# A two-layer decoder trunk: VectorE instead of GpSimd for a layer norm's affine step, ScalarE and GpSimd instead of VectorE for eight convolution taps

## The chip, the cores and the metric

The kernel runs on one core of one Trainium2 chip. The metric is the device time of one execution, in microseconds (us). The engines are named as the profile names them: PE is TensorE (PEld its weight loads), DVE is VectorE, ACT is ScalarE, POOL is GpSimd, SP is SyncE, which issues the DMAs here. Each engine runs its own instructions strictly in the order in which the built program has them, and waits on semaphores for the others.

## The reference

The trunk has two layers over x of 512 tokens and 1024 channels, all in float32. Cut to what matters here:

```
def reference(x, ...):
    for layer in range(2):
        mix = even_mixer(x, ...) if layer % 2 == 0 else odd_mixer(x, ...)
        x = layer_norm(ALPHA * x + mix, ln_mix_g[layer], ln_mix_b[layer])
        x = layer_norm(ALPHA * x + swiglu(x, ffn_w_in[layer], ffn_w_out[layer]),
                       ln_ffn_g[layer], ln_ffn_b[layer])

def odd_mixer(x, w_in, forget_b, dw_w, dw_b, cn_g, cn_b, w_out):
    p = x @ w_in                      # q, k, v of 8 heads of 64; 8 forget gates; 2 x 512 for the convolution
    log_f = log_sigmoid(p[forget gates] + forget_b)
    y_c = forgetting_attention(q, k, v, log_f)
    y_d = conformer_conv(p[the last 1024], dw_w, dw_b, cn_g, cn_b)
    return concatenate([y_c, y_d]) @ w_out

def forgetting_attention(q, k, v, log_f):   # causal; logits q.k/8 + cum[t] - cum[s]; softmax; times v
def conformer_conv(p_d, ...):
    h = p_d[:, :512] * sigmoid(p_d[:, 512:])
    h = causal_dwconv(h, dw_w) + dw_b       # 31 taps on each of 512 channels
    return silu(layer_norm(h, cn_g, cn_b))  # the norm over channels
```

## The kernel before

**Arithmetic.** Matrix products are made from split operands: each float32 operand is written as a high part, rounded to the type in which TensorE multiplies (`split`, lines 85 to 88: ACT copies, DVE or POOL subtracts), and a low part, the remainder. `mm3` (lines 90 to 93) then sums three products, so the matmuls of a projection stand at lines 91, 92 and 93 in the profile.

**Stages.** The four calls at the end of `trunk` run one after the other: `even_mixer`, `ffn(0)`, `odd_mixer`, `ffn(1)`. In `ffn` a part of the products is made by a Strassen scheme (line 389). The tokens lie in four tiles x_74 to x_77 of 128 tokens by 1024 channels.

**The norm behind the first FFN.** `norm` (lines 210 to 220) leaves the tiles as (x - mean) * rstd, without factor and bias; the transposed copy that the odd mixer's projections read gets them there (`transpose_x`). The residual at the odd mixer's end needs them on the token tiles too. That is the affine step: `late_affine` (lines 203 to 208) calls `affine_steps` (lines 194 to 201), which loads factor and bias (`gb`, 512 KB each, spread over the partitions, line 198) into two buffers of the weight pool `wt`, which has eight, and returns 16 instructions of 128x512, a multiplication and an addition for each half of each tile (line 200). They are given out with a priority that is shifted against program order (`tc.high_priority(offset=-CP)`, CP = 900), as are the convolutions.

**The odd mixer.** It begins with the four column blocks j of the convolution's input. `conv` (lines 737 to 758) makes the 31 taps of one block. The last `GT[j]` of them are made by ACT and POOL: ACT multiplies (lines 753 and 748) and POOL adds each product to `convs` (line 749). `prod` holds two products in each of these blocks, so ACT's product i waits for POOL's sum i - 2. The other taps go on DVE: ACT makes the first in PSUM (line 743), DVE adds the rest in place (line 755) and then the two sums (line 758). With GT = (0, 31, 0, 4), blocks 0 and 2 are wholly DVE's, block 1 wholly ACT's and POOL's, and block 3 is shared. Then come the forget gates, their cumulated sums (`cumulate`, lines 858 to 875, into `aug`), and the values. DVE's last row of `aug` (line 875) goes by DMA into the operand tiles (line 928).

**The eight heads.** Lines 1092 to 1107 write out TensorE's order by hand: for every head the ten steps of SEQ.

```
SEQ = "S0 F0 T0 S1 S2 F1 F2 W T1 F3"
```

S are the scores of the 128-row blocks (b=3; b=2 and 0; b=1), with L945, L946, L947 on PE, the row maxima (L952) and reciprocals (L955) on DVE and the exponentials and scaling (L954, L956) on ACT. T are transposes of the probabilities (L970), T0 those of the head before; they are split into th and tl (L87 on ACT, L88 on DVE). W is the weighted sum of the values (L986). F are quarters of the projection of queries and keys of the head after next (`qk_proj`; its operands are made by L917 and L920 on ACT, L918 and L921 on DVE, and copied across partitions by the DMAs of L922 and L923), or in the last two heads parts of the output projection. The operand tiles are three, qk0 to qk2, used in turn.

Other work hangs on a pair (head, step). `CS = [(4, 0), (4, 6), (5, 0), (5, 6)]` places `conv_stats`, the norm of the convolution over channels: PE transposes (L1005) into the PSUM bank "cv", of which there is one; DVE takes the statistics (L1008, L1009, L168), POOL a power (L169), and DVE normalizes out of the bank (L1011). CW places `conv_swish` (L1025 to L1034), which uses the same bank. XG places the affine step; `extra` holds all of these (lines 1082 to 1088).

**What sets the order.** PE's order here is the written one. On the other engines the scheduler decides, by its own estimates of time and by priority; so the place of an instruction in a queue can differ from where the code gives it out.

Of the kernel before, what the change touches and what calls it, by code (L numbers as in the profile page):

```python
# [45 lines left out]
DFIRST = 2  # L46
DG = 1
XA = 2
XG = (3, 8)
FPOS = 3  # L50
GT = (0, 31, 0, 4)
PRE = "C Q0 A0 Q1 V00 V01 A1 V10 V11"
SEQ = "S0 F0 T0 S1 S2 F1 F2 W T1 F3"
CS = [(4, 0), (4, 6), (5, 0), (5, 6)]
# [7 lines left out]
def trunk(ctx, tc, x, ev_w_in, ev_conv_w, ev_pool_w, ev_pool_scale, ev_w_out, od_w_in,  # L62
# [131 lines left out]
    def affine_steps(g, b, eng):  # L194

        gb = [wtp.tile([P, D], F32, tag="wt", name="gb") for _ in range(2)]
        for dst, v in zip(gb, (g, b)):
            nc.sync.dma_start(dst, v.partition_broadcast(P))
        return [lambda t=t, cs=slice(c * 512, (c + 1) * 512), v=v, op=op:
                eng.tensor_tensor(xs[t][:, cs], xs[t][:, cs], v[:, cs], op=op)  # L200
                for t in range(NT) for c in range(2) for v, op in zip(gb, (ALU.mult, ALU.add))]

    def late_affine(g, b, eng):

        steps = affine_steps(g, b, eng)
        with tc.high_priority(offset=-CP):
            for step in steps:
                step()
# [27 lines left out]
    class OutProj:  # L236
# [13 lines left out]
        def step(self, t, i, ws, part=None):  # L250

            q = slice(t * P, (t + 1) * P)
            for acc, cols in self.accs[t] if part is None else [self.accs[t][part]]:
                for kk in range(2):
                    lh, ll = self.lhs(2 * self.order[i] + kk)
                    mm3(acc, lh[:, q], ll[:, q], ws[0][:, kk, cols], ws[1][:, kk, cols],
                        i == 0 and kk == 0, i == len(self.order) - 1 and kk == 1)
# [461 lines left out]
    def odd_mixer():  # L719
# [3 lines left out]
        V = nc.vector  # L723
        G = nc.gpsimd
        with tc.tile_pool(name="odd", bufs=1) as op:
# [11 lines left out]
            def conv(hp, j):  # L737

                acc, n = convs[:, j, :], KCONV - GT[j]
                tap = lambda i: par[:, j, 4 + i:5 + i]  # L740
# [341 lines left out]
            extra = {}  # L1082
# [2 lines left out]
            for j in range(4):  # L1085
                extra.setdefault(CW[j], []).append(lambda j=j: conv_swish(j))

            extra.setdefault(XG, []).append(lambda: late_affine(ln_ffn_g[0], ln_ffn_b[0], G))
            run = lambda key: [f() for f in extra.get(key, ())]
            ctx2.enter_context(tc.manual_schedule(engines={mybir.EngineType.PE}))  # L1090
            pt, seq = {}, SEQ.split()
# [33 lines left out]
    even_mixer()  # L1125
    ffn(0)
    odd_mixer()
    ffn(1)

# [22 lines left out]
```

## Time and profile before

| | us |
|---|---|
| median of the three runs | 1078.4 |
| the runs | 1077.87, 1078.4, 1086.64 |
| the profiled execution | 1077.13 |
| its span | 1075.4 |
| mean granted clock of TensorE | 0.99 |
| heads 0 to 7, from the first head's rest to the last | about 592 to 680 |

A row of the groups view has line, engine, operation, output<-input, shape and count, then busy time in us and the mean duration in ns, then the idle time of the engine just before and what ended it. In the timeline the columns are start and duration in us, engine, line and operation; a bracket gives the engine's idle time before the instruction and its releaser. A row of the waits view reads: who, waited for whom: us in total, times, longest.

### The profile page before, as it was taken

What the parts mean: (1) busy time and instruction counts of PE and PEld (TensorE: products, weight loads), DVE (VectorE), ACT (ScalarE), POOL (GpSimd) and SP (SyncE); (2) the same over time, 40 slices, a digit from 0 to 9 for tenths busy, and PEclk for the clock granted to TensorE, in tenths of its full rate; (3) what the DMA queues carried; (4) which work ended last, traced back from release to release, by engine and by line L of the source; (5) the groups of instructions that cost most, each with busy time, mean ns of one, the idle gap of its engine ahead of it and who ended that gap; (6) DMA issues with size and microseconds to landing.
All of it is one profiled execution on the core that took longest, in us unless ns stands there. A gap on an engine that the chain in (4) does not pass through costs nothing.

```text
span 1075.4 us, 16367 instructions
## 1 busy us (share of the span) xinstructions
PE 1040.8 (97%) x6649; PEld 934.3 (87%) x6649; DVE 742.5 (69%) x1028; ACT 482.6 (45%) x711; POOL 177.1 (16%) x162
## 2 busy tenths in 40 slices
PE   8999999999799999999999999999999799999997
PEld 8888899899788999988978777889899788999986
DVE  3845476988653788757579978466888663788756
ACT  4433243554321455433576888533555321455420
POOL 1000300000000000012499972710000000000003
PEclk9999999999899999999999999999999899999999
DMA  6523502530423340460333332411530433340522
GB/s 197 148 84 113 157 1 63 174 99 21 157 98 118 119 136 21 137 177 21 80 86 91 96 104 59 121 36 42 183 110 2 163 111 117 118 138 21 164 72 79
DMA packets 112457, 108.49 MB, mean 101 GB/s; under 512 B 5256, under 2 KB 93880, under 8 KB 112382
## 3 DMA queue, kind: packets, MB, share of 16 engines
q1 hardware_dynamic: 110462, 105.35, 31.8%
q10 hardware_dynamic: 1920, 2.10, 0.6%
q8 instruction: 52, 0.85, 0.3%
q14 instruction: 23, 0.19, 0.1%
HBM read 103.17 MB, written 2.10 MB: 98 GB/s over the span
## 4 chain that ended last, share of the span: by engine, by line
PE 76%; DVE 10%; ACT 5%; issue 3%; DMA 2%; POOL 2%; ACTq 0%; SPq 0%; POOLq 0%; DVEq 0%
PE fl L389 13%; PE fl L91 8%; PE fl L93 8%; PE fl L92 8%; PE sc L389 6%; PE sc L93 5%; PE sc L92 5%; PE sc L91 5%; DVE sw L381 4%; DVE sum L370 2%; PE py L92 2%; PE py L91 2%; PE py L93 2%; PE cv L93 2%; PE cv L91 2%
## 5 line engine op out<-in xcount | busy, mean ns | idle before, releaser
L87 ACT ACTIVATE w<-raw 128x1024 fp32r<-128x1024 f32 x104 | 109.4, 1058 | 197.4 <-PE sc L92 64.2
L389 PE MATMUL fl<-T,sw 128*128 128x256 f32 x1296 | 162.0, 281 | 14.2 <-ACT u L397 11.1
L389 PEld LDWEIGHTS fl<-T,sw 128*128 128x128 f32 x1296 | 155.5, 191 | 16.8 <-ACT u L397 12.2
L88 DVE TENSOR_TENSOR w<-raw,w 128x1024 fp32r<-128x1024 f32 x77 | 93.9, 1223 | 84.0 <-ACT w L87 83.4
L88 POOL TENSOR_TENSOR w<-raw,w 128x1024 fp32r<-128x1024 f32 x27 | 64.9, 2415 | 417.9 <-ACT w L87 404.2
L377 ACT ACTIVATE sw<-sum 128x1024 fp32r<-128x1024 f32 x72 | 76.1, 1062 | 102.9 <-DVE sum L370 77.3
L381 DVE TENSOR_TENSOR sw<-sum,sw 128x1024 fp32r<-128x1024 f32 x72 | 87.8, 1219 | 24.7 <-ACT sw L377 24.7
L389 PE MATMUL sc<-xh,sw 128*128 128x256 f32 x576 | 104.5, 277 | 0.0
L389 PEld LDWEIGHTS sc<-xh,sw 128*128 128x128 f32 x576 | 89.7, 188 | 0.1
L381 DVE TENSOR_TENSOR sw<-q,sw 128x1024 fp32r<-128x1024 f32 x54 | 65.4, 1220 | 29.2 <-ACT sw L377 29.1
L389 PE MATMUL sc<-xl,sw 128*128 128x256 f32 x288 | 79.8, 277 | 0.0
L169 POOL TENSOR_TENSOR rs<-rs,neghalf 128x1 f32<-128x1 f32 x20 | 13.6, 678 | 401.8 <-DVE rs L168 401.8
L377 ACT ACTIVATE sw<-q 128x1024 fp32r<-128x1024 f32 x54 | 56.4, 1051 | 44.2 <-DMA q<-in_ffn_w_in 44.2
L91 PE MATMUL fl<-w,hh 128*128 128x512 f32 (+1 forms) x176 | 67.8, 385 | 0.5 <-ACT w L87 0.5
L93 PE MATMUL fl<-w,hl 128*128 128x512 f32 (+1 forms) x176 | 67.6, 384 | 0.0
L92 PE MATMUL fl<-w,hh 128*128 128x512 f32 (+1 forms) x176 | 67.6, 384 | 0.0
L755 DVE SCALAR_TENSOR_TENSOR cv<-hp,par,cv 128x512 f32<-128x512 f32 x84 | 63.1, 751 | 5.8 <-ACT cv L743 4.5
L370 DVE TENSOR_TENSOR sum<-q,q 128x1024 f32<-128x1024 f32 x36 | 43.9, 1218 | 25.5 <-DMA q<-in_ffn_w_in 25.5
L91 PE MATMUL sc<-xh,w 128*128 128x256 f32 (+1 forms) x168 | 55.1, 332 | 0.0
L92 PE MATMUL sc<-xl,w 128*128 128x256 f32 (+1 forms) x168 | 55.0, 329 | 0.0
L389 PE MATMUL fl<-xh,sw 128*128 128x256 f32 x288 | 53.2, 279 | 1.9 <-DVE sw L381 1.9
L93 PE MATMUL sc<-xh,w 128*128 128x256 f32 (+1 forms) x168 | 54.8, 328 | 0.0
(419 smaller groups left out, 2638.8 us busy)
## 6 DMA issues: line engine op xcount, KB each, us to landing
q<-in_ffn_w_in SPq DMA_DIRECT2D x72, 512.0 KB
raw<-in_ffn_w_out SPq DMA_DIRECT2D x44, 512.0 KB
raw<-in_od_w_in SPq DMA_DIRECT2D x20, 512.0 KB
raw<-in_ffn_w_in SPq DMA_DIRECT2D x16, 512.0 KB
raw<-in_ev_w_in SPq DMA_DIRECT2D x15, 512.0 KB
raw<-in_ev_w_out SPq DMA_DIRECT2D x8, 512.0 KB
raw<-in_od_w_out SPq DMA_DIRECT2D x8, 512.0 KB
qk<-qk SPq DMA_DIRECT2D x16, 128.0 KB
```

The costliest lines, as they stand in the source:

```text
L87: nc.scalar.activation(hi, src, AF.Copy)
L88: (eng or nc.vector).tensor_tensor(lo, src, f32(hi), op=ALU.subtract)
L91: nc.tensor.matmul(acc, lh, rh, start=start, stop=False)
L92: nc.tensor.matmul(acc, lh, rl, start=False, stop=False)
L93: nc.tensor.matmul(acc, ll, rh, start=False, stop=stop)
L169: nc.gpsimd.tensor_tensor(rs[:, 1:2], rs[:, 0:1], neghalf, op=ALU.pow)
L370: nc.vector.tensor_tensor(raw[name], raw[a], raw[b], op=ALU.add)
L377: nc.scalar.activation(g["A"][name][0], g["raw"][self.LEFT[name]], AF.Copy)
L381: nc.vector.tensor_tensor(lo, g["raw"][self.LEFT[name]], f32(hi), op=ALU.subtract)
L389: nc.tensor.matmul(acc, l[:, k, cols], r[:, k, :], start=start and i == k == m == 0, stop=stop and i == 1 and k == 3 and m == 2, skip_grou ...
L755: V.scalar_tensor_tensor(acc if i == KCONV - 1 else part, hp[:, i:i + S], tap(i), part, op0=ALU.mult, op1=ALU.add)
```

## The change

Two numbers and one engine change:

```
-XG = (3, 8)
+XG = (6, 8)
 FPOS = 3
-GT = (0, 31, 0, 4)
+GT = (0, 31, 0, 12)
...
-            extra.setdefault(XG, []).append(lambda: late_affine(ln_ffn_g[0], ln_ffn_b[0], G))
+            extra.setdefault(XG, []).append(lambda: late_affine(ln_ffn_g[0], ln_ffn_b[0], V))
```

V is VectorE and G is GpSimd. The affine step is now given out behind step 8 of head 6 instead of head 3, and on VectorE. In block 3 of the convolution twelve taps instead of four are made by ACT and POOL, and 18 instead of 26 products are added by DVE (line 755). No other line changes.

## The prediction

> **What bounds the kernel now.** First the page's busy times, then TensorE's idle time by stage in the windows view, then TensorE's waits in the odd mixer.
>
> ```profile
> span 1075.4 us, 16367 instructions
> PE 1040.8 (97%) x6649; PEld 934.3 (87%) x6649; DVE 742.5 (69%) x1028; ACT 482.6 (45%) x711; POOL 177.1 (16%) x162
> ```
>
> ```profile
> 580.00:592.40 12.40, 9.32 (x77) 8.68 (x75) 10.12 (x18) 8.25 (x16) 11.89 (x10) 1.00 0.33 86
> 592.40:632.40 40.00, 38.51 (x199) 30.85 (x200) 35.58 (x79) 34.09 (x85) 37.47 (x31) 0.96 0.27 79
> 632.40:680.00 47.60, 44.52 (x257) 35.93 (x257) 37.14 (x88) 40.16 (x92) 15.89 (x12) 1.00 0.26 80
> 680.00:800.00 120.00, 117.92 (x777) 107.19 (x776) 84.37 (x114) 53.42 (x75) 20.94 (x12) 1.00 0.35 106
> ```
>
> ```profile
> PE sc L947 <- DMA qk<-aug: 3.1, 1, 3.1
> PE tp L970 <- ACT pr L956: 1.5, 4, 0.6
> PE cv L1005 <- DVE sm L955: 0.6, 1, 0.6
> ```
>
> TensorE (PE) is busy for 97% of the span and its order is the same in both kernels, so the time moves only by what makes PE wait. The columns of a windows row are the stretch, its length, then busy time of PE, PEld, DVE, ACT, POOL, the granted clock, and DMA. In heads 0 to 3 (592.4 to 632.4) PE idles 40.00 - 38.51 = 1.5 us, in heads 4 to 7 (to 680) 3.1 us. More than that nothing can be won here. GpSimd (POOL) and VectorE (DVE) are the full engines of heads 0 to 3: 37.5 and 35.6 of 40 us.
>
> **The change, part by part.** It takes eight taps of conv j=3 and the 16 affine steps and swaps their engines.
>
> ```profile
> L749 POOL TENSOR_TENSOR convs<-convs,prod 128x512 f32<-128x512 f32 x33 | 42.5, 1297 | 3.1 <-ACT prod L748 2.0 <-PE fl L92 0.3
> L748 ACT ACTIVATE prod<-hp,par 128x512 f32<-128x512 f32 x33 | 23.5, 719 | 9.4 <-POOL convs L749 9.3
> L755 DVE SCALAR_TENSOR_TENSOR cv<-hp,par,cv 128x512 f32<-128x512 f32 x84 | 63.1, 751 | 5.8 <-ACT cv L743 4.5
> L200 DVE TENSOR_TENSOR x<-x,gb x32: 681/684/695, 288.7 to 873.5; 128x512 f32<-128x512 f32 x32
> L200 POOL TENSOR_TENSOR x<-x,gb x16: 1269/1282/1295, 605.4 to 627.9; 128x512 f32<-128x512 f32 x16
> ```
>
> Work on DVE: 8 x 0.751 = 6.0 us less before head 2, and 16 x 0.65 = 10.4 us more later. Here 0.65 us is the step of back-to-back affine instructions, from the row of six below: (3.94 - 0.68) / 5. On POOL: 16 x 1.28 = 20.5 us less, 8 x 1.30 = 10.4 us more. On ScalarE (ACT): 8 x 0.72 = 5.8 us more. Were the engines free where this falls, PE would notice nothing. Where it falls decides.
>
> **Head 4, the large term.** The schedule puts the sixteen L200 not in the last heads, but into head 4, all between the statistics of the first conv transposes (L1008) and the instruction that reads their PSUM bank for the last time (L1011). DVE before, from L1008 on (qk is an operand tile, tl the low half of a transposed probability block, x_74 to x_77 the four token tiles):
>
> ```order
> L1008 BN_STATS cst<-cv 128x6
> L955 RECIPROCAL sm<-sm 128x1
> L1009 BN_AGGR mv<-cst 128x2
> L168 TENSOR_SCALAR rs<-mv 128x1
> L921 TENSOR_TENSOR qk_5265<-fl,qk_5265 64x512
> L952 TENSOR_REDUCE nm<-sc 128x1
> L88 TENSOR_TENSOR tl<-tp,th 128x512
> L88 TENSOR_TENSOR tl<-tp,th 128x384
> L955 RECIPROCAL sm<-sm 128x1
> L952 TENSOR_REDUCE nm<-sc 128x1 x2
> L1011 TENSOR_SCALAR npair<-cv,mv,rs 128x512
> ```
>
> The same place on DVE in the changed kernel, its first part:
>
> ```order
> L955 RECIPROCAL sm<-sm 128x1
> L200 TENSOR_TENSOR x_74<-x_74,gb 128x512 x2
> L1009 BN_AGGR mv<-cst 128x2
> L200 TENSOR_TENSOR x_75<-x_75,gb 128x512
> L921 TENSOR_TENSOR qk_5273<-fl,qk_5273 64x512
> L200 TENSOR_TENSOR x_75<-x_75,gb 128x512
> L200 TENSOR_TENSOR x_76<-x_76,gb 128x512 x2
> L200 TENSOR_TENSOR x_77<-x_77,gb 128x512 x2
> L952 TENSOR_REDUCE nm<-sc 128x1
> L200 TENSOR_TENSOR x_74<-x_74,gb 128x512
> L168 TENSOR_SCALAR rs<-mv 128x1
> L88 TENSOR_TENSOR tl<-tp,th 128x512
> ```
>
> And DVE's rows that follow directly:
>
> ```order
> L200 TENSOR_TENSOR x_74<-x_74,gb 128x512
> L88 TENSOR_TENSOR tl<-tp,th 128x384
> L200 TENSOR_TENSOR x_75<-x_75,gb 128x512 x2
> L200 TENSOR_TENSOR x_76<-x_76,gb 128x512 x2
> L200 TENSOR_TENSOR x_77<-x_77,gb 128x512 x2
> L955 RECIPROCAL sm<-sm 128x1
> L952 TENSOR_REDUCE nm<-sc 128x1
> L1011 TENSOR_SCALAR npair<-cv,mv,rs 128x512
> ```
>
> Sixteen steps now stand ahead of the second L955 and of L1011. Behind them wait the softmax of the remaining rows of head 4, and PE: the conv bank has one buffer, so PE's second set of conv transposes (the L1005 ahead of the weighted sum, L986) can't start until L1011 has read the first, and PE runs in order. In the trace of before this wait is already without slack:
>
> ```profile
> 632.46 0.40 PE L945 MATMUL sc<-qk 128*128 128x512 f32 x1
> 633.05 0.60 PE L1005 MATMUL cv<-ident,convs 128*128 128x128 f32 x4
> ...
> 640.31 0.63 PE L1005 MATMUL cv<-ident,convs 128*128 128x128 f32 x4 [0.61 <-DVE sm L955]
> ```
>
> ```profile
> 635.84 0.16 DVE L955 RECIPROCAL sm<-sm 128x1 f32<-128x1 f32 x1 [0.45 <-ACT pr L954]
> ...
> 636.46 0.69 DVE L921 TENSOR_TENSOR qk<-fl,qk 64x512 fp32r<-64x512 f32 x1 [0.19 <-ACT qk L920]
> 637.18 0.56 DVE L952 TENSOR_REDUCE nm<-sc 128x1 f32<-128x384 f32 x1
> 637.70 1.16 DVE L88 TENSOR_TENSOR tl<-tp,th 128x512 fp32r<-128x512 f32 x2
> 638.77 0.15 DVE L955 RECIPROCAL sm<-sm 128x1 f32<-128x1 f32 x1
> 638.84 0.60 DVE L952 TENSOR_REDUCE nm<-sc 128x1 f32<-128x128 f32 x2
> 639.36 0.81 DVE L1011 TENSOR_SCALAR npair<-cv,mv,rs 128x512 f32<-128x512 f32 x1
> ```
>
> L1011 ends at 640.17, and PE goes on at 640.31, 0.14 us later. (The wait's named releaser, L955, ended nearby; the bank's reader fits by code and by time.)
>
> When may the first L200 start? The factors come by DMA into buffers of the eight-deep weight pool, and the queue of SP now issues them behind other heads' transfers (qk_5271 to qk_5273 belong to heads 0/3/6, 1/4/7, 2/5). Before, on SP:
>
> ```order
> L98 DMA raw<-in_od_w_out 128x2x512
> L928 DMA qk_5263<-aug 2x512 x2
> L198 DMA gb<-in_ln_ffn_g 128x1024
> L198 DMA gb<-in_ln_ffn_b 128x1024
> L922 DMA qk_5265<-qk_5265 64x512
> ```
>
> SP in the changed kernel:
>
> ```order
> L923 DMA qk_5272<-qk_5272 64x512
> L928 DMA qk_5271<-aug 2x512 x2
> L198 DMA gb<-in_ln_ffn_g 128x1024
> L198 DMA gb<-in_ln_ffn_b 128x1024
> L922 DMA qk_5273<-qk_5273 64x512
> ```
>
> They moved from ahead of head 2's operand copies to ahead of head 5's. Their buffers held the weights of head 5, so they wait for the last projection of head 3, as they waited in before for the last of head 0:
>
> ```profile
> 601.20 0.34 SPq L198 DMA_DIRECT2D gb<-in_ln_ffn_g  x1
> 601.24 0.39 PE L945 MATMUL sc<-qk 128*128 128x512 f32 x1
> 605.44 1.29 POOL L200 TENSOR_TENSOR x<-x,gb 128x512 f32<-128x512 f32 x1 [0.90 <-DMA gb<-in_ln_ffn_g]
> 868.04 3.94 DVE L200 TENSOR_TENSOR x<-x,gb 128x512 f32<-128x512 f32 x6
> ```
>
> Issue lay 0.04 us before the next head's first scores, first use 4.24 us later. Head 4's scores start at 632.46, so L200 starts at 632.42 + 4.24 = 636.66, which is 0.8 us behind L955 and costs DVE little. From there L1011 ends after 16 x 0.65 + 0.1 (L1009) + 0.72 (L921) + 0.52 (L952) + 0.1 (L168) + 1.07 (two tl) + 0.07 (L955) + 0.26 (one L952) + 0.81 = 14.05 us, at 650.71. PE restarts at 650.85 instead of 640.31: **+10.5 us**. Nothing covers it: all that PE could do meanwhile stands behind the L1005. Bounds: below, 16 x 0.65 less the 1.9 us that DVE idled in head 4 (8.5); above, another 1.5 us if the DMA meets the output projection's loads (12.0).
>
> **The clock after it.** A pause of this length isn't in the trace; the nearest are 3.1 and 5.5 us.
>
> ```profile
> 592.32 0.50 PE L947 MATMUL sc<-qk 68*128 68x512 f32 x1 [3.08 <-DMA qk<-aug]
> 275.83 0.58 PE L389 MATMUL fl<-T,sw 128*128 128x256 f32 x1 [5.53 <-ACT u L397]
> 275.83:279.40 3.57, 3.57 (x17) 3.57 (x18) 3.57 (x4) 0.89 (x1) 0.00 (x0) 0.54 0.62 213
> 592.32:596.76 4.44, 4.44 (x17) 3.43 (x17) 3.82 (x8) 2.80 (x6) 4.36 (x5) 0.62 0.35 100
> ```
>
> After them the granted clock was 0.54 over 3.57 us and 0.62 over 4.44 us: 3.57 x 0.46 = 1.6 and 4.44 x 0.38 = 1.7 us lost. I take **+1.7**; bounds 0 (the slowed matmuls lie beside a wait for softmax) and 2.
>
> [...]
>
> **Heads 0 to 3, the small terms.** ACT around the cumulated forget gates (aug) has one tap more ahead of L874, whose output DVE finishes and a DMA carries to PE, which waited 3.08 us for it. Before, on ACT:
>
> ```order
> L872 ACTIVATE aug<-py 8x512
> L748 ACTIVATE prod<-hp,par 128x512
> L743 ACTIVATE cv<-hp,par 128x512
> L87 ACTIVATE wqh<-raw 128x8x64 x2
> L874 ACTIVATE aug<-py 8x512
> ```
>
> ACT in the changed kernel:
>
> ```order
> L872 ACTIVATE aug<-py 8x512
> L748 ACTIVATE prod<-hp,par 128x512
> L743 ACTIVATE cv<-hp,par 128x512
> L87 ACTIVATE wqh<-raw 128x8x64 x2
> L748 ACTIVATE prod<-hp,par 128x512
> L874 ACTIVATE aug<-py 8x512
> ```
>
> ```profile
> 586.90 0.71 ACT L748 ACTIVATE prod<-hp,par 128x512 f32<-128x512 f32 x1
> 587.51 0.76 ACT L743 ACTIVATE cv<-hp,par 128x512 f32<-128x512 f32 x1
> ```
>
> The step from one to the next is 587.51 - 586.90 = 0.61, so **+0.6**. For the rest I take **0**: DVE's relief can return the 1.5 us of idle in these heads, and eight more L748, in line with the softmax on ACT, can cost as much; the bounds are -1.5 and 8 x 0.66 = +5.3, with 0.66 = 9.3 us in 14 waits of L748 for POOL. The near end is likelier: POOL loses its affine between those taps.
>
> **Sum.** 10.5 + 1.7 + 0.6 = 12.8 us. The profiled execution took 1077.13 us (span 1075.4 and 1.7 around it): 1077.1 + 12.8 = 1089.9, say **1090.0**. It lies 1.3 us under the median of before (1078.4), inside the runs' own scatter.
>
> **Rivals.** (1) *The pause is partly repaid*: while PE stands, ACT, POOL and the loads catch up, and the waits behind it vanish. For it: PE idles 3.1 us in heads 4 to 7 (0.6 of it the wait that grows) and 2.1 from 680 to 800. Against it: most are chains through the same one bank, not backlog. At most 2.5 + 2.1 = 4.6 back: 1085.3. (2) *ScalarE and GpSimd pace the first heads*: every L748 waits for the sum two taps earlier, with softmax queued behind it on ACT. For it: POOL at 37.5 of 40 us; against it: DVE is freer just there. 12.8 + 5.3 gives 1095. (3) *Not slower*: the affine is covered. This needs PE to come to its second L1005 of head 4 only at about 650, so that DVE's 14 us pass beside other PE work; then the relief stays, -1.5, and the time is 1075.6. Against it: PE stood there at 639.7, 0.6 us early, and conv work before head 4 would have to be 10 us late. That the title's "last heads" were true would also cover some, but the order shows head 4.
>
> **How the numbers follow.** Forecast 0.68, partly repaid 0.14, paced 0.12, covered 0.06. The forecast's own bounds are about 1087 to 1093; the range is widened to 1084.5 and 1095.0 for (1) and (2). A measurement of this kernel can tell about 1%, that is 10.8 us, from no change: the forecast lies 1 us beyond that line. Two thirds of its chance (0.46) and all of "paced" (0.12) are slower by over 1%, 0.6 rounded; covered gives faster by at most 0.3%, so faster by over 1% gets 0.02, and 0.38 is left for within 1%.
>
> **What the changed profile would show.** One wait of PE L1005 for DVE of about 11 us at 640 to 651, a dozen or more L200 on DVE just before it, PE clock near 0.6 for four us after it; the wait for qk<-aug at 3.7; PE's idle in heads 0 to 3 within 1.5 us of now. It would be wrong if that L1005 waits under 8 us, if the affine runs in another head, or if ACT's waits for convs grow by 5 us with PE behind them.

## The result, and the profile after

| | before | after |
|---|---|---|
| median of the runs, us | 1078.2 (6 runs, 1077.47 to 1086.64) | 1091.9 (6 runs, 1090.24 to 1095.03) |
| the profiled execution, us | 1077.13 | 1090.53 |
| its span, us | 1075.4 | 1088.8 |

The change makes the kernel slower: the ratio of the times is 1.0116, with a 95% interval of 1.0083 to 1.0149 (the two medians alone would give 1.0127). The medians differ by 13.6 us, the profiled executions by 13.4.

The page's head and its rows of the moved work show that the work went where the change says: VectorE has the 16 affine steps more and 8 L755 less, GpSimd the reverse, ScalarE 8 L748 more.

```profile
span 1088.8 us, 16388 instructions
PE 1043.5 (96%) x6649; PEld 937.7 (86%) x6649; DVE 747.5 (69%) x1036; ACT 487.2 (45%) x719; POOL 167.0 (15%) x154
...
L755 DVE SCALAR_TENSOR_TENSOR cv<-hp,par,cv 128x512 f32<-128x512 f32 x76 | 57.1, 752 | 5.8 <-ACT cv L743 4.5
```

VectorE's busy time grew by 5.0 us in 747, and TensorE's share of the span fell by one point. Nothing in these averages looks like 13 us. The windows view by stage does: the same stages as in the prediction, from the first heads to head 4, and then the stretch from TensorE's restart to the first scores of head 5.

```profile
593.00:633.70 40.70, 38.34 (x200) 31.03 (x200) 30.55 (x70) 37.00 (x90) 28.41 (x22) 0.96 0.29 86
633.70:651.15 17.45, 7.24 (x43) 5.65 (x41) 15.74 (x32) 6.24 (x13) 1.47 (x2) 0.79 0.23 76
651.15:655.99 4.84, 4.84 (x21) 4.41 (x22) 3.10 (x9) 2.60 (x8) 2.00 (x2) 0.69 0.35 112
```

TensorE idles 2.4 us of heads 0 to 3 (1.5 before) and 10.2 of 17.45 us in head 4, where VectorE is busy for 15.7. The waits view of TensorE for the odd mixer names it:

```profile
PE cv L1005 <- DVE npair L1011: 10.2, 1, 10.2
PE sc L947 <- DMA qk<-aug: 3.8, 1, 3.8
PE sc L945 <- ACT pr L954: 1.2, 1, 1.2
...
PE sc L945 <- DMA qk<-qk: 0.8, 1, 0.8
```

One wait of 10.2 us has taken the place of one of 0.6; the wait for aug grew by 0.7, and two small ones are new. VectorE's timeline in head 4 shows what L1011 stood behind (start, duration, instruction; in brackets the idle time and its releaser):

```profile
636.55 0.14 DVE L955 RECIPROCAL sm<-sm 128x1 f32<-128x1 f32 x1
637.80 1.29 DVE L200 TENSOR_TENSOR x<-x,gb 128x512 f32<-128x512 f32 x2 [1.11 <-DMA gb<-in_ln_ffn_g]
...
640.41 3.09 DVE L200 TENSOR_TENSOR x<-x,gb 128x512 f32<-128x512 f32 x5
643.53 0.56 DVE L952 TENSOR_REDUCE nm<-sc 128x1 f32<-128x384 f32 x1
...
646.33 3.69 DVE L200 TENSOR_TENSOR x<-x,gb 128x512 f32<-128x512 f32 x6
649.94 0.15 DVE L955 RECIPROCAL sm<-sm 128x1 f32<-128x1 f32 x1
650.01 0.27 DVE L952 TENSOR_REDUCE nm<-sc 128x1 f32<-128x128 f32 x1
650.20 0.80 DVE L1011 TENSOR_SCALAR npair<-cv,mv,rs 128x512 f32<-128x512 f32 x1
```

And TensorE's timeline at the same place:

```profile
633.70 0.40 PE L945 MATMUL sc<-qk 128*128 128x512 f32 x1
...
640.55 0.39 PE L93 MATMUL fl<-xh,wql 128*128 128x512 f32 x1
651.15 1.08 PE L1005 MATMUL cv<-ident,convs 128*128 128x128 f32 x4 [10.21 <-DVE npair L1011]
```

Factor and bias are there 4.10 us after head 4's first scores; from then on VectorE is never idle until L1011 ends at 651.00, and TensorE goes on 0.15 us later. The four L1005 now take 1.08 us instead of 0.63. The windows view in steps of a microsecond, whose column of the clock is the one after POOL's, shows why: half the clock for 3 us, then all of it.

```profile
651.10:652.10 1.00, 0.95 (x5) 0.98 (x6) 0.44 (x3) 0.74 (x3) 1.00 (x1) 0.50 0.00 0
652.10:653.10 1.00, 1.00 (x5) 0.90 (x5) 0.82 (x3) 0.57 (x2) 0.50 (x1) 0.50 0.06 16
653.10:654.10 1.00, 1.00 (x6) 1.00 (x6) 0.30 (x3) 0.00 (x0) 0.55 (x1) 0.50 0.31 37
654.10:655.10 1.00, 1.00 (x7) 0.82 (x7) 0.75 (x1) 0.60 (x1) 0.00 (x0) 0.96 0.92 338
```

### The profile page after: what moved, and what is told of

Read it like the earlier page. It is cut to its first block, busy times and chain, and to the rows that moved or that the text cites. A ratio compares the mean times of both kernels' runs of the same rounds, so it can differ in the third digit from the quotient of the medians.

```text
span 1088.8 us, 16388 instructions
## 1 busy us (share of the span) xinstructions
PE 1043.5 (96%) x6649; PEld 937.7 (86%) x6649; DVE 747.5 (69%) x1036; ACT 487.2 (45%) x719; POOL 167.0 (15%) x154
## 4 chain that ended last, share of the span: by engine, by line
PE 73%; DVE 13%; ACT 5%; DMA 4%; issue 3%; POOL 1%; ACTq 0%; SPq 0%; POOLq 0%; DVEq 0%
PE fl L389 11%; PE fl L91 8%; PE fl L92 8%; PE fl L93 8%; PE sc L389 5%; PE sc L91 5%; PE sc L92 5%; PE sc L93 5%; DVE sw L381 5%; DVE sum L370 3%; PE py L91 2%; PE py L92 2%; PE py L93 2%; ACT sw L377 2%; PE cv L91 2%
## 5 line engine op out<-in xcount | busy, mean ns | idle before, releaser
L389 PE MATMUL fl<-T,sw 128*128 128x256 f32 x1296 | 162.4, 282 | 13.4 <-ACT u L397 10.6
L169 POOL TENSOR_TENSOR rs<-rs,neghalf 128x1 f32<-128x1 f32 x20 | 13.6, 678 | 417.3 <-DVE rs L168 417.3
L755 DVE SCALAR_TENSOR_TENSOR cv<-hp,par,cv 128x512 f32<-128x512 f32 x76 | 57.1, 752 | 5.8 <-ACT cv L743 4.5
```

What stands on the lines that cost most here:

```text
L169: nc.gpsimd.tensor_tensor(rs[:, 1:2], rs[:, 0:1], neghalf, op=ALU.pow)
L389: nc.tensor.matmul(acc, l[:, k, cols], r[:, k, :], start=start and i == k == m == 0, stop=stop and i == 1 and k == 3 and m == 2, skip_grou ...
L755: V.scalar_tensor_tensor(acc if i == KCONV - 1 else part, hp[:, i:i + S], tap(i), part, op0=ALU.mult, op1=ALU.add)
```

## The experiments

Each kernel was timed beside runs of the kernel before on the same chip; their median was 1077.6 us beside E1 to E4, 1081.3 beside E5 to E8, 1078.1 beside E9 and E10, and 1079.9 beside E11 and E12. So each is given as a ratio to these runs, and the places are compared by the starts of the first scores (L945, 128x512) of each head in the profiled executions. Head 0 has its first scores at 570 us, ahead of the gates' sums, so the first column holds more than four heads' work. What lies ahead of them is in no column; it takes 569.7 to 574.3 us, and the profiles differ by it too.

| us | heads 0 to 3 | head 4 | heads 5 and 6 | head 7 to the end | ratio of the times (95%) |
|---|---|---|---|---|---|
| before | 62.2 | 11.3 | 23.9 | 407.8 | 1 |
| after | 63.4 | 22.3 | 23.9 | 409.0 | 1.0116 (1.0083 to 1.0149) |
| E1 affine step alone | 61.0 | 23.1 | 23.9 | 409.0 | 1.0124 (1.0105 to 1.0143) |
| E2 taps alone | 61.0 | 27.3 | 23.9 | 411.7 | 1.0151 (1.0134 to 1.0168) |
| E3 half the steps | 63.9 | 18.3 | 23.9 | 408.4 | 1.0101 (1.0084 to 1.0117) |
| E4 bank used later | 63.5 | 20.7 | 29.5 | 408.6 | 1.0176 (1.0147 to 1.0204) |
| E5 GpSimd, head 4 | 63.7 | 21.7 | 30.2 | 408.5 | 1.0180 (1.0148 to 1.0213) |
| E6 VectorE, head 6 | 65.0 | 10.5 | 34.8 | 409.5 | 1.0122 (1.0093 to 1.0151) |
| E7 GpSimd, heads 5 to 7 | 63.8 | 10.5 | 24.9 | 417.8 | 1.0078 (1.0050 to 1.0106) |
| E8 the same, yc moved, 4 taps | 61.7 | 10.5 | 24.9 | 415.1 | 1.0054 (1.0031 to 1.0078) |
| E9 VectorE, behind the heads | 64.6 | 10.5 | 23.9 | 418.3 | 1.0104 (1.0085 to 1.0122) |
| E10 the same, 4 taps | 61.1 | 10.5 | 23.9 | 417.5 | 1.0076 (1.0056 to 1.0095) |
| E11 the same, yc on GpSimd | 61.4 | 10.5 | 23.9 | 414.7 | 1.0050 (1.0031 to 1.0069) |
| E12 E10, GpSimd idle beside | 60.7 | 11.0 | 26.8 | 420.0 | 1.0104 (1.0084 to 1.0123) |

### E1 and E2: each part alone

E1 against the changed kernel, E2 against the kernel before:

```
-GT = (0, 31, 0, 12)
+GT = (0, 31, 0, 4)
```

```
-GT = (0, 31, 0, 4)
+GT = (0, 31, 0, 12)
```

> The affine step alone goes to VectorE and to (6, 8); block 3 of the convolution keeps its four taps on ScalarE and GpSimd. Theory (sixteen L200 in VectorE's line ahead of L1011 in head 4): the order has the same sixteen steps at the same place, so TensorE waits 9.5 to 11 us at the second L1005, the clock gives up 1.4 us behind it, and the time is 1077.1 + 9.6 + 1.4 = 1088, about 10 to 12 us above the kernel before. Rival A (the added taps make most of the loss): the time stays within 4 us of before, 1077 to 1081. Rival B (both parts are needed, because VectorE only has no slack with both): no clear number, but the wait at the second L1005 stays under 5 us.

> Eight more taps of block 3 go to ScalarE and GpSimd; the affine step stays on GpSimd at (3, 8). Theory (an engine's order sets the end): GpSimd now has the sixteen L200 (20.5 us) ahead of its last taps in its line, 10.4 us more work up to the first L1005 than in the kernel before, where it was busy for 37.5 of 40 us; five of its additions stand behind two weight splits that ended at 637.7 before. So the first L1005 of head 4 waits for the convolution, 8 to 14 us, and the time is 1085 to 1092. Rival A (the eight taps by themselves are harmless where they go, as heads 0 to 3 of the changed kernel lost only 1.2 us): 1077 to 1080, no wait of an L1005 over 2 us.

E1 has the same wait to a tenth, and the ratio 1.0124 is that of the whole change. TensorE's timeline of E1:

```profile
652.70 1.09 PE L1005 MATMUL cv<-ident,convs 128*128 128x128 f32 x4 [10.16 <-DVE npair L1011]
```

Both rivals fall: neither are the taps most of the loss, nor are both parts needed. The theory's 1088 was low by 3.6 us against the median 1091.6; the clock took 2.3 us here (658.44 - 652.70 = 5.74 us from the restart to the first scores of head 5, against 643.76 - 640.31 = 3.45 before), and the profiled execution was 4 us late before the heads began (574.26 against 570.31). Whether the other executions were late there too is not known.

E2 is slower still. GpSimd's timeline and TensorE's wait:

```profile
637.04 1.29 POOL L749 TENSOR_TENSOR convs<-convs,prod 128x512 f32<-128x512 f32 x1
638.27 2.35 POOL L88 TENSOR_TENSOR w<-raw,w 128x1024 fp32r<-128x1024 f32 x1
640.57 5.30 POOL L749 TENSOR_TENSOR convs<-convs,prod 128x512 f32<-128x512 f32 x4
```

```profile
645.92 0.90 PE L1005 MATMUL cv<-ident,convs 128*128 128x128 f32 x3 [13.97 <-POOL convs L749]
```

The last sums end at 645.87, and the first L1005 of head 4 waits 13.97 us for them, the upper end of the 8 to 14 expected. The median, 1094.1, lies 2 us over the 1085 to 1092 expected: the clock is at half for 5.6 us behind this wait, and the stretch from head 7 to the end is 3.9 us longer than before, which was not traced. Each part by itself loads one in-order line ahead of head 4; the change as a whole exchanges GpSimd's line for VectorE's.

### E3: half the steps

This kernel leaves factor and bias off the tiles x_76 and x_77; it is here only for its waits. Of the changed kernel:

```
-            for step in steps:
+            for step in steps[:8]:
```

> The changed kernel with the affine step on the first two token tiles only (tiles x_76 and x_77 get neither factor nor bias at this place): eight L200 of 0.65 us less in VectorE's line in head 4, none of the transfers less. Theory (the wait is the sum of the steps in line): the wait at the second L1005 falls by 8 x 0.65 = 5.2 us to 5.0 us; the clock still falls behind it and costs 1.4; the time is 5.2 us under the changed kernel, 1085.3 beside its 1090.5. Rival C (the late arrival of factor and bias sets the wait, not the number of steps): the wait stays above 8 us and the time within 2 us of the changed kernel. Rival D (a pause of 5 us costs no clock): the time is 6.6 us under the changed kernel.

TensorE's timeline of E3:

```profile
647.43 1.09 PE L1005 MATMUL cv<-ident,convs 128*128 128x128 f32 x4 [5.67 <-DVE npair L1011]
```

The wait fell by 10.21 - 5.67 = 4.54 us: eight steps of 0.60 us are 4.8, and factor and bias came 0.3 later behind the first scores (638.91 - 634.52 = 4.39). Rival C falls. Rival D falls too: from the restart to the next head's scores it takes 652.84 - 647.43 = 5.41 us, 1.96 more than before, though the pause was half as long. The loss by steps follows their number, the loss by the clock doesn't. The median, 1088.4, is 3.5 us under the changed kernel's, where 5.2 were expected.

### E4: the bank needed later

Of the changed kernel:

```
-CS = [(4, 0), (4, 6), (5, 0), (5, 6)]
+CS = [(4, 0), (5, 0), (5, 4), (5, 7)]
```

> The changed kernel with the second to fourth set of convolution transposes moved from (4, 6), (5, 0), (5, 6) to (5, 0), (5, 4), (5, 7): TensorE doesn't need the one cv bank again in head 4, while VectorE's line is as in the changed kernel. Theory as the prediction has it (L1011 and the bank carry the wait): TensorE no longer waits in head 4, and the time comes back to 1079 to 1082. Rival E (the block of steps stops the softmax and the splits of the same line just as well, the bank is only the first to show it): TensorE waits for the splits tl (end at 646.4 in the changed kernel) ahead of the weighted sum and for the scaled probabilities ahead of the next transposes (651.0), 7 us in sum instead of 10.2, and the time is about 3.3 us under the changed kernel, 1087.

TensorE's waits in the odd mixer:

```profile
PE py L986 <- DVE tl L88: 5.5, 1, 5.5
...
PE tp L970 <- ACT pr L956: 2.7, 2, 2.4
PE cv L1005 <- DVE npair L1011: 1.9, 1, 1.9
PE cv L1025 <- DVE npair L1011: 1.6, 1, 1.6
```

Without the bank in its way TensorE stops all the same, 5.5 us for the splits tl and 2.4 for the probabilities, both in or behind VectorE's line. Head 4 is only 1.6 us shorter (20.7 against 22.3). Rival E is borne out. Its time, 1087, is not: the median is 1096.6. Heads 5 and 6 pay 5.6 us for the new places of the conv_stats; the waits of 1.9 and 1.6 us for L1011 above are new with them, and the rest was not traced. So the ratio says nothing on the bank; the waits do.

### E5: the engine put back, the place kept

Of the changed kernel:

```
-            extra.setdefault(XG, []).append(lambda: late_affine(ln_ffn_g[0], ln_ffn_b[0], V))
+            extra.setdefault(XG, []).append(lambda: late_affine(ln_ffn_g[0], ln_ffn_b[0], G))
```

> The changed kernel with only the engine of the affine step put back: it stays at (6, 8), but runs on GpSimd. Theory (what counts is what stands in line behind the sixteen steps, not which engine does them): GpSimd's line has eight L200 ahead of the power L169 that L1011 of the first conv_stats needs, and eight more ahead of the second L169. With factor and bias at 637.8, the first L169 runs at 647.9, L1011 ends at 649.3 and TensorE waits 8.5 us at the second L1005; the second L169 runs at 658.5 and the third L1005 waits about 5 us. With two drops of the clock the time is 1090 to 1095, no better than the changed kernel. Rival (VectorE's load is the cause, GpSimd is idle in these heads): neither wait over 2 us, 1077 to 1080.

GpSimd's timeline, and the two L1005 of TensorE's:

```profile
638.91 9.87 POOL L200 TENSOR_TENSOR x<-x,gb 128x512 f32<-128x512 f32 x8 [10.37 <-DMA gb<-in_ln_ffn_g]
648.73 0.56 POOL L169 TENSOR_TENSOR rs<-rs,neghalf 128x1 f32<-128x1 f32 x1
649.25 9.90 POOL L200 TENSOR_TENSOR x<-x,gb 128x512 f32<-128x512 f32 x8
```

```profile
650.28 1.09 PE L1005 MATMUL cv<-ident,convs 128*128 128x128 f32 x4 [8.64 <-DVE npair L1011]
660.65 1.08 PE L1005 MATMUL cv<-ident,convs 128*128 128x128 f32 x4 [3.83 <-DVE npair L1011]
```

Expected were 8.5 and about 5 us. GpSimd was idle for 10.4 us before its first step, and it still holds TensorE up, since a power of 0.56 us stands in line behind ten microseconds of additions. It isn't VectorE's load. The time is worse than the 1090 to 1095 expected: 1.0180 of the kernel before. Heads 5 and 6 take 6.3 us more than before, of which the wait of 3.83 us is a part.

### E6: the steps on VectorE in head 6

Of the changed kernel:

```
-XG = (6, 8)
+XG = (8, 0)
...
-        with tc.high_priority(offset=-CP):
+        with ExitStack():
```

> The changed kernel with the affine step given out behind head 7 (XG = (8, 0)) and without the shifted priority; it stays on VectorE. The built order has the sixteen L200 in head 6, between the two L1030, which read the same one cv bank for conv_swish. Theory: the wait moves there with them: no wait over 1 us at the second L1005 of head 4, and in head 6 one of 8 to 11 us at an L1025, with the clock at half for 3 to 5 us behind it; the time is 1087 to 1092. Rival (head 4 is the only place without slack; further back VectorE is freer): no wait over 3 us in head 6 and 1077 to 1081.

```profile
668.70 0.80 PE L91 MATMUL fl<-w,yc 128*128 128x512 f32 x1 [5.80 <-DVE qk L921]
...
676.58 1.09 PE L1025 MATMUL cv<-ident,npair 128*128 128x128 f32 x4 [2.61 <-DVE zconv L1030]
```

TensorE's timeline in head 6 shows these two waits, 8.4 us together; the rival falls. Head 4 has none left (10.5 us), and heads 5 and 6 are 10.9 us longer than before: the loss moved with the steps, as the theory has it. The instruction that shows it first is another than expected: L921, a part of the operand tiles, stands in the line too, and TensorE meets it before the bank.

### E7 and E8: the steps on GpSimd behind the conv_stats

E7 is E6 with G for V. E8 is E7 with these two edits:

```
-GT = (0, 31, 0, 12)
+GT = (0, 31, 0, 4)
...
-                    split(yc[j // 2][:, j % 2, 0, :], yc[j // 2][:, j % 2, 1, :], y32[j], G if j < 3 else V)
+                    split(yc[j // 2][:, j % 2, 0, :], yc[j // 2][:, j % 2, 1, :], y32[j], G if j < 2 else V)
```

> As the run before it, with the affine step on GpSimd: the built order has the sixteen L200 behind all four L169 of conv_stats, where GpSimd was idle for 8.1 and 11.6 us in the kernel before; the twelve taps stay. Theory: no conv_stats waits for them; what stands behind is one split of yc (L88), which TensorE needs at about 676: with L200 from 658.5 it comes at 679, so a wait of about 3 us in the output projection; with the 1.2 us of heads 0 to 3 the time is 1078 to 1082. Rival (the eight added taps cost more than the 1.2 us once VectorE's steps no longer hide it): over 1084.

> As the run before it, with the split of yc of heads 4 and 5 moved from GpSimd to VectorE, so that it doesn't stand behind the affine step, and with the four taps of the kernel before. Theory: nothing that TensorE waits for stands behind the sixteen L200 any more, GpSimd is rid of 20.5 us in heads 0 to 3, and at most the 1.5 us of TensorE's idle time there come back: 1075.5 to 1077.5, which can't be told from the kernel before. Rival (GpSimd's load in heads 0 to 3 is what delays the softmax and the loads, and more than these heads profit): under 1073.

Both theories were too good: 1.0078 and 1.0054 instead of 1.001 to 1.005 and about 0.999. The heads to head 6 cost little, the loss is from head 7 on: 10.0 us in E7, 7.3 in E8. E7's rival meets its figure (over 1084) but hardly its reason: heads 0 to 3 are 1.6 us longer than before with twelve taps and 0.5 shorter with four, so the taps are about 2 of the 10. E8's rival, under 1073, falls. In E8, one row each of ScalarE's and TensorE's timeline, and two of the groups view from 658 to 683:

```profile
671.19 1.06 ACT L87 ACTIVATE w<-raw 128x1024 fp32r<-128x1024 f32 x1 [3.07 <-POOL x L200]
```

```profile
674.83 0.58 PE L945 MATMUL sc<-qk 128*128 128x256 f32 x1 [2.52 <-ACT pr L954]
```

```profile
L200 POOL TENSOR_TENSOR x<-x,gb 128x512 f32<-128x512 f32 x16 | 23.9, 1528 | 5.3 <-DMA gb<-in_ln_ffn_g 5.3
L1033 DVE SCALAR_TENSOR_TENSOR yconv<-yconv,zconv 128x512 f32<-128x512 f32 x4 | 5.4, 1359 | 3.0 <-ACT zconv L1032 3.0
```

Three things were not in my account. A weight copy on ScalarE, into a buffer of the pool `wt` that holds the factors too, waits 3.07 us for the eighth L200, and has the softmax of head 7 behind it in line, so TensorE waits 2.52 us. Behind this wait the granted clock is 0.52 over 6.96 us (674.83 to 681.79), so the clock takes up to 6.96 x 0.48 = 3.3 us, more than the wait. And the engines slow each other: GpSimd's sixteen steps take 23.9 us instead of 20.1, and L1033 on VectorE 1.36 us instead of the 0.69 that it takes in the kernel before. E12 comes back to this.

### E9 and E10: the steps on VectorE behind the heads

E9 against the changed kernel; E10 is E9 with GT = (0, 31, 0, 4):

```
-XG = (6, 8)
+XG = (8, 2)
...
-        with tc.high_priority(offset=-CP):
+        with ExitStack():
...
-                proj.first(3, g)
+                proj.first(3, g); g == B and run((NH, 2))
```

> The changed kernel (affine step on VectorE, twelve taps) with the affine step given out behind the last part of the output projection (proj.first(3)) and without the shifted priority. The built order has the sixteen L200 behind the last L991, ahead of the residual additions L177; there VectorE was idle for 2.3 and 4.6 us in the kernel before and for 21.5 of 50 us from 680 to 730. Theory (the loss is what stands in line behind the steps): ten of the changed kernel's 12.2 us up to head 7 go, TensorE has no wait over 1.5 us from head 4 on, and there remain the 1.2 us of heads 0 to 3: 1.001 of before, 1077 to 1080 where before takes 1077. Rival A (sixteen steps on VectorE cost TensorE their 10 us wherever they stand in the odd mixer): 1.010 or more. Rival B (the weight splits of the second FFN, which take over the two buffers of factor and bias, come late): a wait of 3 us or more for a w in ffn(1), 1.003 to 1.006.

> As the run before it, with the four taps of the kernel before. Theory: neither VectorE's line in head 4 nor GpSimd's in heads 0 to 3 holds the affine step, and ScalarE has no more taps than before; heads 0 to 3 take 0.5 to 1.1 us less than before, as in the runs with four taps and the affine step elsewhere (61.0 and 61.7 us from the first scores of head 0 to those of head 4, against 62.2). The time is 0.999 to 1.000 of before, not to be told from it. Rival A: 1.010 or more. Rival B: 1.003 to 1.006.

The theory's 1.001 and 1.000 are wrong: 1.0104 and 1.0076. Rival B's wait for a w didn't come. Rival A's figure is met in E9, but not its reason, since TensorE's wait is 5.2 us and has a cause of its own at this place. VectorE's timeline of E10 and TensorE's wait:

```profile
682.66 14.09 DVE L200 TENSOR_TENSOR x<-x,gb 128x512 f32<-128x512 f32 x8 [0.61 <-DMA gb<-in_ln_ffn_g]
696.67 0.68 DVE L88 TENSOR_TENSOR yc<-yatt,yc 128x512 fp32r<-128x512 f32 x1
697.27 4.89 DVE L200 TENSOR_TENSOR x<-x,gb 128x512 f32<-128x512 f32 x8
```

```profile
697.40 0.80 PE L93 MATMUL fl<-w,yc 128*128 128x512 f32 x1 [5.20 <-DVE yc L88]
```

Eight steps take 14.09 us and the next eight 4.89. The first eight lie beside GpSimd's weight splits (GpSimd is busy for 11.9 us from 682.6 to 696), the others beside an idle GpSimd (0.0 from 696 to 702.2). The split of yc stands behind the slow eight. So the theory of the line holds (something awaited did stand behind), but the price of a step was wrong by a factor of nearly three at this place (1.76 us against 0.65), and I had not looked at what else is in that line.

### E11 and E12: the split of yc out of the line, and GpSimd out of the way

E11 and E12 against E10:

```
-                    split(yc[j // 2][:, j % 2, 0, :], yc[j // 2][:, j % 2, 1, :], y32[j], G if j < 3 else V)
+                    split(yc[j // 2][:, j % 2, 0, :], yc[j // 2][:, j % 2, 1, :], y32[j], G)
```

```
-                    ws = [load_cols(w_in, c * DFF + i * P, eng=nc.gpsimd) for i in range(FIRST) for c in range(2)]
+                    ws = [load_cols(w_in, c * DFF + i * P, eng=nc.vector if l else nc.gpsimd) for i in range(FIRST) for c in range(2)]
...
-            proj = OutProj(od_w_out[0], [0, 2, 3, 1], lhs, 4, lambda kp: [next(spare), next(spare)], eng=G)
+            proj = OutProj(od_w_out[0], [0, 2, 3, 1], lhs, 4, lambda kp: [next(spare), next(spare)], eng=V)
```

> As the run with the affine step on VectorE behind the heads and four taps, with one more edit: the split of yc of heads 6 and 7 goes from VectorE to GpSimd. In that run TensorE waited 5.2 us for this split, which stood behind eight L200 that took 14.1 us together. Theory (the sixteen steps cost nothing once nothing that TensorE awaits stands behind them): the split is done by about 689 in GpSimd's line, before TensorE asks for it at 692; no wait over 1.5 us in the output projection, no drop of the clock there, and the time is 5.2 us of wait and about 2 us of clock less than 1086.6: 1079 to 1080, or 0.999 to 1.002 of before. Rival (the next thing in VectorE's line, the residual additions L177 that start 12 us late, then holds TensorE): a wait of 3 us or more for L177's banks or for xl and xt, 1.004 or more.

> As the run with the affine step on VectorE behind the heads and four taps, with the weight splits (L88, w) of the odd mixer's output projection and of the first blocks of the second FFN moved from GpSimd to VectorE, so that GpSimd has no large work beside the sixteen L200. Theory (VectorE's additions of two SBUF operands and GpSimd's instructions keep each other out): no L200 takes over 0.8 us, the sixteen 10.9 us together instead of 19.0, although VectorE has some 9 us more work around them. Rival (transfers, or ScalarE's reading, slow them): some L200 still take 2 to 3 us. The time is not the question here.

E11 gets rid of the wait for yc, and the rival takes its place. VectorE's timeline, one row of GpSimd's, then TensorE's:

```profile
682.61 20.10 DVE L200 TENSOR_TENSOR x<-x,gb 128x512 f32<-128x512 f32 x16 [0.53 <-DMA gb<-in_ln_ffn_g]
702.64 0.67 DVE L177 SCALAR_TENSOR_TENSOR x<-x,fl 128x512 f32<-128x512 f32 x1
```

```profile
687.68 8.46 POOL L88 TENSOR_TENSOR w<-raw,w 128x1024 fp32r<-128x1024 f32 x3
```

```profile
703.36 0.50 PE L91 MATMUL fl<-w,yc 128*128 128x512 f32 x1 [1.11 <-DVE x L177]
...
711.00 1.11 PE L135 MATMUL tp<-ident,x 128*128 128x128 f32 x8 [3.44 <-DVE x L218]
```

The residual additions start at 702.6 instead of 689.4, and the norm behind them is late for TensorE by 3.4 us. At 1.0050 it is the nearest of all to the kernel before, and still slower.

E12 decides on the slow steps. The source view of L200 has the minimum, median and maximum duration in ns; first E11, with GpSimd's splits beside the steps, then E12, without them:

```profile
L200 DVE TENSOR_TENSOR x<-x,gb x16: 673/678/2892, 682.6 to 702.0; 128x512 f32<-128x512 f32 x16
```

```profile
L200 DVE TENSOR_TENSOR x<-x,gb x16: 680/683/692, 685.7 to 699.0; 128x512 f32<-128x512 f32 x16
```

Without GpSimd's splits no step takes over 0.69 us, with more work on VectorE. The rival falls by the windows view too. Transfers: the first two steps of the changed kernel, beside an idle GpSimd, take 1.29 us together at a DMA share of 0.90 (637.8 to 639.1), and in E10 one step fills the two microseconds from 690 to 692 at 0.60, beside a GpSimd that is busy throughout. ScalarE: it is idle in E11 from 692.0 to 696.2, where two steps take 4.2 us; its weight copy waits 6.7 us for an L200 there. The time, 1.0104, with the splits in VectorE's line, was not the question.

No run beats the kernel before.

## Why the prediction was right, point by point

**The sum.** +12.8 us were predicted. The profiled executions differ by 13.4, of which 12.2 had come about by the first scores of head 7 (679.84 against 667.65). The other 1.2 us came behind it (409.0 us from there to the end against 407.8), from the second FFN on, where neither kernel was changed. The runs of the kernel before scatter by more (1077.75 to 1082.64 beside E11), so I count it as scatter; its cause was not traced. E1, E3, E4 and E5 have 408.4 to 409.0 there, so the 407.8 may be the odd one. That the sum is only 0.6 us off is partly luck: head 4 and the clock were put 1.2 us too high, the first heads and this stretch 1.8 too low. The mechanism and the two large terms are not luck.

**Head 4, +10.5.** Measured: TensorE's restart moved from 640.31 to 651.15, 10.84 us, of which 1.24 were there before head 4. That leaves 9.6, inside the bounds (8.5 to 12.0). The start of the steps was right (4.10 us behind the first scores, 4.20 predicted); the size of a step was 0.05 us too large: (3.69 - 0.68) / 5 = 0.60, times 16 is 0.8 us. E1 shows that this part alone makes the loss, E3 that it goes with the number of steps, E5 and E6 that it goes with the place and not with the engine.

**The bank.** The prediction named both the softmax and the bank behind the steps, but put the wait on the bank's second use, and reckoned it as if that were the one reason. E4 shows that the bank only shows it first: without it 7.9 us of 10.2 stay, for tl and the probabilities. For this change the number is the same; for a mending it is not, since freeing the bank won 1.6 us in head 4.

**The clock, +1.7.** Measured 655.99 - 651.15 - 3.45 = 1.4 here, 2.3 in E1 and 2.0 in E3. The size was right, the upper bound of 2 a little low.

**Heads 0 to 3.** The chain of aug was expected at +0.6 and took +0.7 (3.8 against 3.1). The rest was put at 0 and took 0.5: the waits for pr (1.2) and for qk (0.8) are new, some of those of L970 went. The zero was a difference of two larger things, as the runs without the affine step in these heads show: with four taps 61.1 us (E10), with twelve 63.4 (after), with four and the affine step on GpSimd 62.2 (before). The relief was worth 1.1 us, the eight taps cost 2.3. That comparison is of profiled executions of different kernels, one each. It doesn't add up for every pair: E2, with twelve taps and the affine step on GpSimd, takes 61.0 us here; there the last sums come in head 4, and the loss with them. So the 2.3 us are shown only for an affine step that isn't in GpSimd's line.

**The rivals.** *Partly repaid*: heads 5 and 6 take 23.9 us before and after; nothing was paid back. *Paced by ScalarE and GpSimd*: the waits of L748 for convs fell, as this row of the page's groups shows (9.3 us before), so the waits that this rival goes by did not grow. A small part of it is there all the same: an added L748 of 0.72 us, at 615.41, stands in ScalarE's line right ahead of the L954 for which TensorE waits 1.2 us.

```profile
L748 ACT ACTIVATE prod<-hp,par 128x512 f32<-128x512 f32 x41 | 28.9, 717 | 6.5 <-POOL convs L749 6.5
```

*Covered*: it would have needed TensorE to come to head 4's second L1005 at 650; it came at 640.9. E6 to E11 tried to find such cover further back, and found a line with something awaited behind it each time.

## What to carry to other kernels

An addition of 0.6 us on an engine that is 69% busy can cost the bound engine its full length, where an awaited instruction stands behind it in an in-order line (eight steps of 0.60 us less were 4.54 us less of waiting in E3); so read the order at the place, list everything that stands behind, and find who asks for it and when, before looking at shares. Moving the work to a less busy engine or a later place may only change which instruction is late: each arrangement tried here had one (L1011, the power L169, L921, a weight copy into the same pool, yc, the norm). Price a step with what the neighbour engine does at that moment, because its duration isn't a constant (an L200 took 0.68 us beside an idle GpSimd and up to 2.89 beside its weight splits).

## What the runs showed of the hardware that I had not expected

**VectorE's L200 and GpSimd's weight splits slow each other.** An L200 on VectorE, two operands in SBUF, takes 0.68 us beside an idle GpSimd (the kernel before, 855.2 to 873.5) and up to 2.89 beside GpSimd's weight splits (E11); with these splits elsewhere the maximum is 0.69 (E12). The splits take 2.8 us each beside the steps (8.46 for three in E11) and 2.4 ahead of them and behind. The profile books the time as the instruction's duration and not as a wait, so no row of waits shows it: E10's eight steps of 14.09 us have 0.61 us of idle time before them. L755 keeps its 0.75 us beside a GpSimd that is 94% busy (heads 0 to 3 before); its accumulator is in PSUM, but no run shows whether that is the reason. In head 4 of the changed kernel GpSimd was busy for 1.5 of 17.45 us, and a step took 0.60 us there, close to the 0.65 of the prediction.

**The clock fell after a pause of 5 us as after one of 10, and stayed at half for different times**: 4.2 us after E3's pause of 5.67, 3.0 us after the changed kernel's of 10.2, 4.9 after E1's equal one, and in E2, after 14.0 us, five full windows of 1 us at 0.50 and a sixth at 0.69, 5.6 us in all:

```profile
649.90:650.90 1.00, 1.00 (x6) 0.89 (x4) 0.00 (x0) 0.60 (x1) 0.00 (x0) 0.50 0.00 0
650.90:651.90 1.00, 1.00 (x7) 0.87 (x6) 0.69 (x1) 0.49 (x1) 0.00 (x0) 0.69 0.00 0
```

No run shows what sets these times. Short pauses don't go by their length either: behind the 2.52 us of E8 the clock was 0.52 for 6.96 us, behind the 3.44 us of E11 it stayed at 1.00.
